# Router weights made at the last projection and in the first mixture, and the first tile's router work in steps between the last products, in a two-layer decoder trunk

## Chip, cores and metric

One core of a Trainium2 chip runs the whole program. The metric is the device time of one execution in microseconds, lower is better. TensorE (PE) multiplies; its weight loads are listed as PEld. VectorE is DVE, ScalarE is ACT, GpSimd is POOL, SyncE is SP. Each engine takes its instructions strictly in the order in which they stand in the program; SP does nothing here but issue the large transfers, one after the other, each when the buffer it writes is free.

## What is computed

The trunk has two layers over 256 tokens of width 2048, in float32. This is the reference, cut to what matters here:

```python
h = x
for layer in range(2):
    m = retention_conv_mixer(h, ...) if layer == 0 else dsa_mixer(h, ...)   # input projection, mixing, output projection
    h = layer_norm(ALPHA * h + m, mix_ln_g[layer], mix_ln_b[layer])
    f = grouped_moe(h, router_w, router_b, w_gu[layer], w_down[layer])
    h = layer_norm(ALPHA * h + f, ffn_ln_g[layer], ffn_ln_b[layer])

def grouped_moe(x, ...):
    affinity = sigmoid(x @ router_w)                 # 256 x 16: the router
    # best of 4 groups of 4 experts, two experts in it, their affinities scaled to sum 1: gate
    for e in range(16):
        a, b = split(x @ w_gu[e], 2)
        y += gate[:, e] * ((silu(a) * b) @ w_down[e])
```

`router_w` (2048 x 16) is shared by both layers. The layer norm before the router is folded into it: with z the unnormed rows, the router's input is rs * (z @ W) + bias, where W is `router_w` scaled row by row with the layer's `mix_ln_g`, less the mean of each column (so that the mean of z drops out), and the bias is `mix_ln_b @ router_w`. W and the bias are the "router weights" of a layer.

## The kernel before

**Stages.** In order: `even` (input projection of layer 0 with rotary embedding, retention and a 31-tap convolution beside it, then the output projection), `moe(0)` (the first mixture), `odd` (layer 1's projections and sparse attention), `moe(1)`, `final` (last layer norm and stores). Tokens are two tiles of 128 rows, t = 0 and 1.

**Projections.** A projection's weights come in chunks of 1 MB (tiles `w`). A chunk is cut into two units of 128 x 1024 values; `split` makes of each a high half on ACT (line 243) and a low half by a subtraction (line 246, tile `sp`) that stands alternately on DVE and POOL, and `mm` issues three products for each of its two slices and two row tiles (lines 284 to 286): 12 products a unit. `dense` walks the units; `ensure` issues the split of a unit three units ahead of its products. After each unit, `bg` issues pieces of background tasks, as many as a budget of 1.3 allows; a task yields its cost (the convolution's steps, line 525, cost 0.33 each, so about four a unit) or -1, which parks it until the next unit. The last five units (`tail`) are done apart: all products of row tile 0, then `z_done` for it, then the products of row tile 1.

**The router's part.** `router(layer)` made a layer's router weights as a background task: in `even` behind the small loads, in `odd` behind the task that turns rows back. It took a page of 8 KB a partition (`rtmp`), loaded `router_w` into it, multiplied it on DVE with both vectors (line 444), summed over the partitions by a product with ones on PE (`prw`, line 447), and reduced, scaled and subtracted on DVE (lines 450 to 453) into `rw`. Each finished column group of an output projection is turned (`psz`, line 734), copied by ACT (`zt`, line 736) and multiplied with `rw` (`plog`, line 739) by `raw`; `total` sums the partial results (`part` on ACT, line 745; `plg` on PE, line 747; `arg` on DVE, line 748). `moe_begin` is called once in the tail, behind the third of the five units of row tile 1, and does for row tile 0 the last `raw`, the norm (`normed`, lines 772 to 778) and `total` in one go.

**The mixtures.** Experts go in eight pairs i, each as `gu(i, 0)`, `down`, `gu(i, 1)`, `down`: 24 chunks a pair, 192 in all (201 MB). SP issues a chunk when one of the pages of its ring (up to 20) has been read to the end.

**The end.** `final` makes six of the eight output pieces on PE and ACT (tile `res`, line 1499) and two on DVE (tile `z`, line 1503); SP stores each.

Of the kernel before, what the change touches and what calls it, by code (L numbers as in the profile page):

```python
# [10 lines left out]
F32 = mybir.dt.float32  # L11
# [69 lines left out]
class Trunk:  # L81
# [208 lines left out]
    def dense(self, us, between, hooks=None, budget=1.3, ahead=3, tail=5):  # L290
        hooks = hooks or {}
        n = 0
        def ensure(i):
            nonlocal n
            while n < min(len(us), i + min(ahead, i + 3) + 1):
                self.split(us[n])
                for f in hooks.get(("split", n), ()):
                    f()
                n += 1

        for i, u in enumerate(us[:-tail]):
            for f in hooks.get(("pre", i), ()):
                f()
            ensure(i)
            self.mm(u)
            if u["last"]:
                u["g"].done(u["g"].acc)
            for f in hooks.get(i, ()):
                f()
            self.bg(budget)  # L310

        for i, u in enumerate(us[-tail:]):
            ensure(len(us) - tail + i)
            self.mm(u, (0,))
        u["g"].done(u["g"].acc, (0,))
        for i, u in enumerate(us[-tail:]):
            self.mm(u, (1,))
            if i == 2:
                between()
        u["g"].done(u["g"].acc, (1,))  # L320


# [61 lines left out]
    def load_small(self):  # L384
# [15 lines left out]
        def task():  # L400
            for _ in range(10):
                yield -1
            ps = self.psum("psv")
            nc.tensor.transpose(ps[:, 0:P], v, self.ident)
            nc.tensor.transpose(ps[:, P:P + 24], cv, self.ident[:24, :24])
            nc.vector.tensor_copy(self.vecs, ps[:, 0:P])
            nc.vector.tensor_copy(self.cvec, ps[:, P:P + 24])
            ps2 = self.psum("psw").rearrange("p (c t) -> p c t", c=16)
            for c in range(8):
                nc.tensor.transpose(ps2[:, c, :TAPS], cw[:, c * P:(c + 1) * P], self.ident[:TAPS, :TAPS])  # L410
            nc.vector.tensor_copy(self.cw[:, :, :TAPS], ps2[:, 0:8, :TAPS])
            nc.gpsimd.partition_broadcast(self.gng, self.gng[0:1, :])
            self.pool_split = True
            yield 0.6
            nc.gpsimd.dma_start(self.cst[:, P:], self.a["c_misc"][:, P:])
            nc.gpsimd.tensor_copy(self.tri, self.cst[:, C_TRI:C_TRI + P])
            nc.gpsimd.tensor_copy(self.identb, self.ident)
            self.ret = self.page("ret", [P, R_N])
            nc.gpsimd.dma_start(self.ret, a["c_ret"])
            nc.gpsimd.dma_start(self.rb, a["router_b"].rearrange("(o e) -> o e", o=1).to_broadcast([P, 16]))  # L420

            for l in range(2):
                for n, nm in enumerate(("mix_ln_g", "mix_ln_b")):
                    nc.gpsimd.dma_start(self.vp[:, 2 * l + n, :].rearrange("p (q r) -> p q r", q=8), a[nm][l].rearrange("(q p r) -> p q r", p=P, r=2))
            yield -1
            yield from self.router(0)
        self.tasks.append(task())

    def router(self, layer):

        nc = self.nc
        V = nc.vector
        tmp = self.page("rtmp")
        raw = tmp[:, 0:256].rearrange("p (k e) -> p k e", k=16)
        both = tmp[:, 256:768].rearrange("p (n k e) -> p n k e", n=2, k=16)
        sums = tmp[:, 768:800].rearrange("p (n e) -> p n e", n=2)
        one = tmp[:, 1024:1024 + P]
        nc.gpsimd.dma_start(raw, self.a["router_w"].rearrange("(c p) e -> p c e", p=P))
        nc.gpsimd.memset(one, 1.0)
        for _ in range(6):  # L440
            yield -1
        for n in range(2):
            v = self.vecs[:, 32 * n + 16 * layer:32 * n + 16 * layer + 16]
            V.tensor_tensor(both[:, n], raw, v[:, :, None].to_broadcast([P, 16, 16]), ALU.mult)
        yield -1
        ps = self.psum("prw")
        nc.tensor.matmul(ps, one, tmp[:, 256:768], start=True, stop=True)
        yield -1
        for n in range(2):
            V.tensor_reduce(sums[:, n], ps[:, n * 256:(n + 1) * 256].rearrange("p (k e) -> p e k", k=16), AX.X, ALU.add)  # L450
        V.tensor_copy(self.rbias, sums[:, 1])
        V.tensor_scalar(sums[:, 0], sums[:, 0], 1.0 / D, None, op0=ALU.mult)
        V.tensor_tensor(self.rw[:, :, 0:16], both[:, 0], sums[:, 0][:, None, :].to_broadcast([P, 16, 16]), ALU.subtract)
        self.drop()
        yield 0.6

    def halves(self, name):

# [3 lines left out]
    def even(self):  # L462
# [218 lines left out]
        def close_act():  # L681
            est.close()
            self.moe_open(0)
            self.rings(11)
            self.table(AF.Sigmoid)
        hooks = {("pre", n): [start_out], n + 0: [ret_T(0, 0)], n + 1: [ret_T(0, 1)], n + 2: [ret_T(1, 0)],
# [54 lines left out]
    def total(self, t):  # L741

        nc = self.nc
        part = self.mp.tile([P, P], F32, name="part", tag="gtt", bufs=2)
        nc.scalar.activation(part, self.pl[:, t * P:(t + 1) * P], AF.Copy)
        pg = self.psum("plg")[:, 0:16]
        nc.tensor.matmul(pg, part, self.sel, start=True, stop=True)
        nc.vector.scalar_tensor_tensor(self.arg[:, t, :], pg, self.rs[:, t:t + 1], self.rbias, op0=ALU.mult, op1=ALU.add)
# [135 lines left out]
        self.pl = self.psum("plog")  # L884
        self.extra_at = self.first[layer] + 8

    def moe_begin(self):

        self.flush()
        for _ in self.raw(0, 3):  # L890
            pass
        self.normed(0)
        self.total(0)

    def moe(self, layer, before_last=None):
        nc, tc = self.nc, self.tc
# [2 lines left out]
        X, Y, GT = {}, {}, {}  # L899
        self.rings(20)  # L900
        h = self.acc
        for _ in self.raw(1, 3):
            pass
        self.total(1)
        self.route(mp)
        self.gate_parts()

# [194 lines left out]
        for i in range(8):  # L1102
# [31 lines left out]
            def general():  # L1134
                self.overflow(layer, rv, h, wide)
                self.ringmax = 8
                if before_last:
                    before_last()
            also = {6: {1: late((1, 0)), 3: late((1, 1)), 5: late((1, 2)), 7: late((1, 3))},
                    7: {3: general, 5: lambda: begin(2, self.bank), 7: lambda: begin(3, self.psum)}}.get(i)  # L1140
            sl = gu(i, 1, also)
            if i == 6:
                self.drop(2)
# [54 lines left out]
    def odd(self):  # L1198
# [38 lines left out]
                yield -1  # L1237
            self.drop(2)
        self.tasks.append(back())
        self.tasks.append(self.router(1))  # L1240

        t4 = lambda n: ap.tile([P, 2, 512], F32, name=n, tag="t4", bufs=3)
        held = {}
# [222 lines left out]
    def final(self):  # L1466
# [26 lines left out]
        for n, (t, c) in enumerate(shared):  # L1493
# [3 lines left out]
            nc.tensor.matmul(ps[t, c], diag[:, t * P:(t + 1) * P], self.acc[t][:, cut(c)], start=False, stop=True)  # L1497
            o = res[t][:, cut(c)]
            nc.scalar.activation(o, ps[t, c], AF.Copy)
            nc.sync.dma_start(orow[:, t, cut(c)], o)  # L1500
        for t, c in own:
            z = centre(t, c)
            V.scalar_tensor_tensor(z, z, self.rs[:, t:t + 1], b[:, cut(c)], op0=ALU.mult, op1=ALU.add)
            nc.sync.dma_start(orow[:, t, cut(c)], z)

    def build(self):
        self.setup()
# [30 lines left out]
```

## Time and profile before

| | us |
|---|---|
| device time, median of 3 runs (lowest to highest) | 1684.91 (1682.84 to 1686.29) |
| the profiled execution: its own time | 1684.84 |
| its span, first to last instruction | 1683.1 |
| busy in the span: PE / DVE / ACT / POOL | 1634.3 / 793.7 / 528.5 / 359.6 |

The profile is of one execution; 1.74 us of its time lie outside the span. Busy time of PE is modelled from pipelined products and says little of what bounds a stage. The views used below are what the 16 DMA engines moved in slices, tables of stretches, the chain of work that ended last, lists of instructions in order of time, and tables of who waited for whom.

### The profile page before, as it was taken

Reading aid. Unit: us, or ns where it says so; the run is one execution under the profiler, and the core shown is the slowest. Engines: PE = TensorE matmul, PEld = TensorE weight load, DVE = VectorE, ACT = ScalarE, POOL = GpSimd, SP = SyncE. Lnnn points to the kernel's source line nnn. Section 1 sums busy time; section 2 is a strip of 40 time slices with the busy share of each in tenths; the row PEclk is TensorE's granted clock in tenths of the full one; section 3 lists DMA queues with packets and bytes.
Section 4 is the critical chain, followed back from the end, with each engine's and each line's share of the span. In section 5 each row is a group of like instructions: output and inputs, shape, how many; then the busy total and the mean of one; then the engine's idle time right before and its main releaser. Section 6 shows DMA issues by size and latency. Waiting matters only on the chain.

```text
span 1683.1 us, 21370 instructions
## 1 busy us (share of the span) xinstructions
PE 1634.3 (97%) x8449; PEld 1021.2 (61%) x8449; DVE 793.7 (47%) x1467; ACT 528.5 (31%) x852; POOL 359.6 (21%) x247
## 2 busy tenths in 40 slices
PE   9999999998999999999999999999899999999998
PEld 7877887786344444544347788878645444454534
DVE  5699987723132223335246585664313322322624
ACT  5333445443121211121135444554312221212112
POOL 2444554542000000010013544334200000001000
PEclk9999999999999999999999999999999999999999
DMA  9754545948999999999993553447789999999994
GB/s 345 220 175 151 175 134 170 339 172 325 355 411 424 427 426 426 427 426 426 425 331 127 167 183 127 149 151 275 315 343 427 417 427 426 426 426 427 427 425 187
DMA packets 123165, 528.47 MB, mean 314 GB/s; under 512 B 10651, under 2 KB 11171, under 8 KB 74803
## 3 DMA queue, kind: packets, MB, share of 16 engines
q1 hardware_dynamic: 122130, 525.32, 79.3%
q0 software_dynamic: 784, 1.66, 0.4%
q8 instruction: 69, 1.13, 0.3%
q14 instruction: 38, 0.30, 0.0%
q10 hardware_dynamic: 144, 0.07, 0.0%
HBM read 524.91 MB, written 2.10 MB: 313 GB/s over the span
## 4 chain that ended last, share of the span: by engine, by line
PE 80%; DVE 8%; DMA 6%; ACT 3%; issue 1%; POOL 1%; DVEq 0%; ACTq 0%; POOLq 0%; SPq 0%
PE pgu L956 22%; PE pdn L1000 11%; PE acc L284 10%; PE acc L286 10%; PE acc L285 9%; PE psg L916 7%; DMA w<-in_moe_w_gu_dram 4%; PE psa L1019 3%; DVE pcv L525 3%; DMA w<-in_moe_w_down_dram 2%; DVE sp L246 2%; PE pdn L1087 1%; PE acc L263 1%; ACT sp L243 1%; DVE Yl L990 0%
## 5 line engine op out<-in xcount | busy, mean ns | idle before, releaser
L956 PE MATMUL pgu<-w,X 128*64 128x512 f32 x2048 | 451.4, 594 | 2.9 <-DMA w<-in_moe_w_gu_dram 2.9
L246 POOL TENSOR_TENSOR sp<-w,sp 128x1024 fp32r<-128x1024 f32 (+1 forms) x105 | 262.7, 2510 | 295.1 <-ACT sp L243 274.7
L956 PEld LDWEIGHTS pgu<-w,X 128*64 128x64 f32 x2048 | 144.2, 137 | 289.5 <-issue 268.3
L243 ACT ACTIVATE sp<-w 128x1024 fp32r<-128x1024 f32 (+1 forms) x224 | 226.4, 1045 | 104.9 <-PE acc L286 36.2
L246 DVE TENSOR_TENSOR sp<-w,sp 128x1024 fp32r<-128x1024 f32 (+1 forms) x119 | 182.1, 1535 | 138.2 <-ACT sp L243 137.1
L1000 PE MATMUL pdn<-w,gT 128*64 128x512 f32 x944 | 209.1, 595 | 0.0
L990 DVE SCALAR_TENSOR_TENSOR Yl<-pdn,gs,Yh 64x512 fp32r<-64x512 f32 (+1 forms) x124 | 90.8, 733 | 228.8 <-ACT Yh L989 215.1
L989 ACT ACTIVATE Yh<-pdn,gs 64x512 fp32r<-64x512 f32 (+1 forms) x124 | 82.9, 668 | 230.3 <-PE pdn L1000 171.5
L284 PE MATMUL acc<-sp,xhi 128*128 128x512 f32 x384 | 153.2, 399 | 0.0
L285 PE MATMUL acc<-sp,xhi 128*128 128x512 f32 x384 | 150.8, 393 | 1.8 <-DVE sp L246 1.8
L286 PE MATMUL acc<-sp,xlo 128*128 128x512 f32 x384 | 150.4, 392 | 0.0
L1000 PEld LDWEIGHTS pdn<-w,gT 128*64 128x64 f32 x944 | 65.3, 137 | 121.6 <-issue 116.7
L874 POOL CAST pb<-pt 128x256 bf16<-128x256 f32 x16 | 7.0, 436 | 611.7 <-DVE pt L873 506.4
L960 DVE TENSOR_TENSOR sl<-sl,pgu 128x256 f32<-128x256 f32 x32 | 13.5, 421 | 243.1 <-ACT sl L959 243.1
L959 ACT ACTIVATE sl<-pgu 128x256 f32<-128x256 f32 x32 | 12.3, 383 | 358.4 <-PE pgu L956 358.4
L525 DVE SCALAR_TENSOR_TENSOR pcv<-up,cw,pcv 128x255 f32<-128x255 f32 (+14 forms) x240 | 113.1, 471 | 7.3
L923 DVE TENSOR_SCALAR X<-psg,vp 128x128 f32<-128x128 f32 x128 | 52.4, 410 | 107.0 <-ACT X L925 107.0
L284 PE MATMUL acc<-sp,hhi 128*128 128x512 f32 x240 | 99.1, 413 | 0.4 <-ACT hhi L1223 0.4
L286 PE MATMUL acc<-sp,hlo 128*128 128x512 f32 x240 | 93.9, 391 | 0.0
L285 PE MATMUL acc<-sp,hhi 128*128 128x512 f32 x240 | 93.6, 390 | 0.0
L925 ACT ACTIVATE X<-psg,vp 128x128 f32<-128x128 f32 x128 | 58.5, 457 | 99.5 <-PE psg L916 68.8
L285 PEld LDWEIGHTS acc<-sp,xhi 128*128 128x128 f32 x384 | 72.5, 189 | 17.8 <-DVE sp L246 3.1
(332 smaller groups left out, 2224.1 us busy)
## 6 DMA issues: line engine op xcount, KB each, us to landing
w<-in_moe_w_gu_dram SPq DMA_DIRECT2D x256, 1024.0 KB, 18.9
w<-in_moe_w_down_dram SPq DMA_DIRECT2D x126, 1024.0 KB, 19.4
w<-in_even_w_in_dram SPq DMA_DIRECT2D x46, 1024.0 KB, 6.4
w<-in_odd_w_in_dram SPq DMA_DIRECT2D x32, 1024.0 KB, 5.3
w<-in_even_w_out_dram SPq DMA_DIRECT2D x16, 1024.0 KB, 7.5
w<-in_odd_w_out_dram SPq DMA_DIRECT2D x16, 1024.0 KB, 5.1
acc<-in_x_dram SPq DMA_DIRECT2D x8, 256.0 KB, 8.5
w<-in_even_w_in_dram SPq DMA_DIRECT2D x4, 512.0 KB, 6.0
```

The lines of the kernel that those rows point to most:

```text
L243: nc.scalar.activation(sp[:, 0], src, AF.Copy)
L246: eng.tensor_tensor(sp[:, 1], src, sp[:, 0].bitcast(F32), ALU.subtract)
L284: nc.tensor.matmul(ac, xh[:, x], wh, start=st, stop=False)
L285: nc.tensor.matmul(ac, xh[:, x], wl, start=False, stop=False)
L286: nc.tensor.matmul(ac, xl[:, x], wh, start=False, stop=en)
L525: nc.vector.scalar_tensor_tensor(y, up[:, c, 0:S - i], w, y, op0=ALU.mult, op1=ALU.add)
L916: nc.tensor.matmul(ps[:, b * P:(b + 1) * P], f, self.PT[i][0][:, t, :], start=t == 0, stop=t == 1)
L925: nc.scalar.activation(X[i][:, k, :], ps[:, b * P:(b + 1) * P], AF.Identity, bias=sh, scale=g)
L956: nc.tensor.matmul(ps[h * 64:(h + 1) * 64, :], X[i][:, k, j * 64:(j + 1) * 64], wv[:, kk, :, h, :], start=k == 0, stop=k == KT - 1)
L989: nc.scalar.activation(hi, po[r, :], AF.Copy, scale=g)
L990: V.scalar_tensor_tensor(lo, po[r, :], g, hi.bitcast(F32), op0=ALU.mult, op1=ALU.subtract)
L1000: nc.tensor.matmul(po[b][half * 64:(half + 1) * 64, :], gT[:, c, h * 64:(h + 1) * 64], wv[:, half ^ j, 2 * b:2 * b + 2, :], start=kk == 0, ...
```

## The change

The router's weights are loaded straight into `rw` (in `even` with the other small loads, by POOL; for layer 1 again at expert pair 2 of the first mixture). Layer 0's `router` is now a background task that starts when the output projection has begun and the mixture's buffers are open; layer 1's is called in three steps during `gu(3, 1)` of the first mixture. The page `rtmp` is gone. `between` is called behind each of the five units of the tail, and `moe_begin` issues its work in pieces behind the third and the fourth; `total` of row tile 0 ends in `moe`. In `final` the stores stand in another order.

```diff
@@ dense
         for i, u in enumerate(us[-tail:]):
             self.mm(u, (1,))
-            if i == 2:
-                between()
+            between(i)
@@ load_small
             nc.gpsimd.dma_start(self.ret, a["c_ret"])
+            self.router_load()
             nc.gpsimd.dma_start(self.rb, ...)
...
-            yield -1
-            yield from self.router(0)
@@ router
-        tmp = self.page("rtmp")
-        raw = tmp[:, 0:256].rearrange("p (k e) -> p k e", k=16)
...
-        nc.gpsimd.dma_start(raw, self.a["router_w"].rearrange("(c p) e -> p c e", p=P))
+        raw = self.rw[:, :, 0:16]
+        flat = self.mp.tile([P, 512], F32, name="rboth", tag="gtt", bufs=2)
...
+        one = self.mp.tile([P, 256], F32, name="sl", tag="sl", bufs=1)[:, 0:P]
         nc.gpsimd.memset(one, 1.0)
-        for _ in range(6):
-            yield -1
...
+    def router_load(self):
+        self.nc.gpsimd.dma_start(self.rw[:, :, 0:16], self.a["router_w"].rearrange("(c p) e -> p c e", p=P))
@@ even, close_act
             self.moe_open(0)
+            self.tasks.append(self.router(0))
@@ total
+        yield -1
         part = self.mp.tile([P, P], F32, name="part", tag="gtt", bufs=2)
         nc.scalar.activation(part, self.pl[:, t * P:(t + 1) * P], AF.Copy)
+        yield -1
         pg = self.psum("plg")[:, 0:16]
@@ moe_begin
-    def moe_begin(self):
-        self.flush()
-        for _ in self.raw(0, 3):
-            pass
-        self.normed(0)
-        self.total(0)
+    def moe_begin(self, i):
+        if i == 2:
+            self.flush()
+            self.steps = [self.raw(0, 3), self.total(0)]
+            for g in self.steps:
+                next(g)
+            next(self.steps[0])
+            self.normed(0)
+        if i == 3:
+            next(self.steps[0], None)
+            next(self.steps[1])
@@ moe
-        for _ in self.raw(1, 3):
-            pass
-        self.total(1)
+        next(self.steps[1], None)
+        for g in (self.raw(1, 3), self.total(1)):
+            for _ in g:
+                pass
...
+            if layer == 0 and i == 2:
+                self.router_load()
...
+            if layer == 0 and i == 3:
+                steps = self.router(1)
+                also = {c: lambda: next(steps, None) for c in (1, 4, 6)}
             sl = gu(i, 1, also)
@@ odd
-        self.tasks.append(self.router(1))
@@ final
-            nc.sync.dma_start(orow[:, t, cut(c)], o)
+        for k in shared[:2]:
+            store(*k)
         for t, c in own:
...
             nc.sync.dma_start(orow[:, t, cut(c)], z)
+            for k in shared[2 + 2 * t:4 + 2 * t]:
+                store(*k)
```

PE in the tail of the first output projection, before: the products `acc` of row tile 1, and between the third unit and the fourth `psz`, `plog` and `plg` of row tile 0 (`acc_70` is row tile 0, `acc_71` row tile 1).

```order
L286 MATMUL acc<-sp,cclor 128x512
L734 MATMUL psz<-cst,acc_70 128x128 x4
L739 MATMUL plog<-zt,rw 32x128 x4
L747 MATMUL plg<-cst,part 128x16
L284 MATMUL acc<-sp,cchir 128x512
...
L286 MATMUL acc<-sp,cclor 128x512
L734 MATMUL psz<-cst,acc_71 128x128 x4
```

The same place now.

```order
L731 MATMUL psz<-cst,acc_70 128x128 x4
L284 MATMUL acc<-sp,cchir 128x512
...
L286 MATMUL acc<-sp,cclor 128x512
L736 MATMUL plog<-zt,rw 32x128 x4
L284 MATMUL acc<-sp,cchir 128x512
...
L286 MATMUL acc<-sp,cclor 128x512
L746 MATMUL plg<-cst,part 128x16
L731 MATMUL psz<-cst,acc_71 128x128 x4
```

Six products of the fourth unit now stand between `psz` and `plog`, six of the fifth between `plog` and `plg`, and the tail of the second output projection is changed in the same way.

DVE where the convolution begins, before: the subtractions `sp`, the router's work on `rtmp`, and the convolution's steps on `pcv`.

```order
L246 TENSOR_TENSOR sp<-w_378,sp 128x1024
L444 TENSOR_TENSOR rtmp<-rtmp,vecs 128x256 x2
L527 TENSOR_SCALAR pcv<-up,cw,cvec 128x256 x2
L525 SCALAR_TENSOR_TENSOR pcv<-up,cw,pcv 128x255 x2
L246 TENSOR_TENSOR sp<-w_439,sp 128x1024
L450 TENSOR_REDUCE rtmp<-prw 128x16 x2
L451 COPY rbias<-rtmp 128x16
L452 TENSOR_SCALAR rtmp<-rtmp 128x16
L453 TENSOR_TENSOR rw<-rtmp 128x16x16
L525 SCALAR_TENSOR_TENSOR pcv<-up,cw,pcv 128x254 x2
...
L246 TENSOR_TENSOR sp<-w_471,sp 128x1024
```

The same place now.

```order
L246 TENSOR_TENSOR sp<-w_378,sp 128x1024
L523 TENSOR_SCALAR pcv<-up,cw,cvec 128x256 x2
L521 SCALAR_TENSOR_TENSOR pcv<-up,cw,pcv 128x255 x2
L246 TENSOR_TENSOR sp<-w_437,sp 128x1024
L521 SCALAR_TENSOR_TENSOR pcv<-up,cw,pcv 128x254 x2
...
L521 SCALAR_TENSOR_TENSOR pcv<-up,cw,pcv 128x251 x2
L246 TENSOR_TENSOR sp<-w_469,sp 128x1024
```

The router's seven instructions have left this stretch, and the convolution stands two steps further on at the next subtraction.

ACT some 40 us later, where the first finished pair of convolution channels (`pcv`) is copied to `cy`, before.

```order
L499 ACTIVATE sg<-acc 128x512 x2
L243 ACTIVATE sp<-w_687 128x1024
L243 ACTIVATE sp<-w_729 128x1024 x2
L529 ACTIVATE cy<-pcv 128x512
L243 ACTIVATE sp<-w_769 128x1024 x2
```

The same place now.

```order
L495 ACTIVATE sg<-acc 128x512 x2
L243 ACTIVATE sp<-w_678 128x1024
L243 ACTIVATE sp<-w_720 128x1024
L525 ACTIVATE cy<-pcv 128x512
L243 ACTIVATE sp<-w_720 128x1024
```

The copy to `cy` has moved ahead of one high half of a split.

## Rows read from the trace of the kernel before

**Rows 1.** The page: the span, and what the DMA engines moved in 40 equal slices of it.

```profile
span 1683.1 us, 21370 instructions
GB/s 345 220 175 151 175 134 170 339 172 325 355 411 424 427 426 426 427 426 426 425 331 127 167 183 127 149 151 275 315 343 427 417 427 426 426 426 427 427 425 187
```

**Rows 2.** Table of stretches at the start of the first mixture, and one row at the start of the second: length, busy time of PE, PEld, DVE, ACT and POOL with counts, granted TensorE clock (1.00 is 2.4 GHz), share of the DMA engines, GB/s.

```profile
416.00:420.00 4.00, 4.00 (x25) 4.00 (x24) 1.18 (x6) 0.91 (x2) 0.00 (x0) 0.63 1.01 428
420.00:424.00 4.00, 4.00 (x22) 1.46 (x20) 1.10 (x3) 0.91 (x2) 0.00 (x0) 1.00 0.49 184
424.00:428.00 4.00, 4.00 (x28) 2.63 (x28) 0.69 (x2) 0.91 (x2) 0.00 (x0) 1.00 0.97 365
476.00:480.00 4.00, 4.00 (x22) 1.29 (x19) 2.25 (x3) 2.19 (x4) 0.00 (x0) 1.00 0.91 342
...
1222.00:1226.00 4.00, 4.00 (x21) 1.44 (x20) 0.96 (x3) 0.91 (x2) 0.00 (x0) 1.00 0.52 197
```

**Rows 3.** The chain of work that ended last, near the end of the first mixture: start, length, what.

```profile
778.06 21.09 DMA w<-in_moe_w_gu_dram
...
818.73 19.55 DMA w<-in_moe_w_gu_dram
```

**Rows 4.** The same chain in the tail of the first output projection.

```profile
386.38 0.57 PE plog L739 x16
...
400.60 0.23 PE acc L286
400.83 0.45 PE psz L734 x4
401.30 0.60 ACT zt L736
401.90 1.40 ACT acc L776 x2
403.30 0.17 ACT part L745
403.52 0.40 PE plg L747 x2
403.91 0.33 PE acc L284
406.79 0.70 DVE acc L719
```

**Rows 5.** The same chain in the tail of the second output projection.

```profile
1203.76 1.40 ACT z L776 x2
```

**Rows 6.** DVE in order of time where the convolution begins: start, length, instruction, count, and in brackets the idle time before it and what ended it.

```profile
57.39 0.69 DVE L500 TENSOR_TENSOR sg<-sg,ga 128x512 f32<-128x512 f32 x1 [0.67 <-ACT sg L499]
61.78 0.75 DVE L444 TENSOR_TENSOR rtmp<-rtmp,vecs 128x256 f32<-128x256 f32 x2
65.76 2.51 DVE L246 TENSOR_TENSOR sp<-w,sp 128x1024 fp32r<-128x1024 f32 x1 [0.26 <-ACT sp L243]
68.19 0.74 DVE L450 TENSOR_REDUCE rtmp<-prw 128x16 f32<-128x256 f32 x2
70.67 2.51 DVE L453 TENSOR_TENSOR rw<-rtmp 128x256 f32<-128x256 f32 x1
73.11 3.08 DVE L525 SCALAR_TENSOR_TENSOR pcv<-up,cw,pcv 128x254 f32<-128x254 f32 x6
```

**Rows 7.** DVE, POOL and ACT in order of time, 30 us further on (three lists, one after the other), and last the subtractions on DVE from 66 to 114 us as one group: count, busy time in us, mean ns of one, idle time before them.

```profile
103.86 5.69 DVE L500 TENSOR_TENSOR sg<-sg,ga 128x512 f32<-128x512 f32 x2
113.31 1.22 DVE L246 TENSOR_TENSOR sp<-w,sp 128x1024 fp32r<-128x1024 f32 x1
...
103.70 5.30 POOL L246 TENSOR_TENSOR sp<-w,sp 128x1024 fp32r<-128x1024 f32 x2 [10.90 <-ACT sp L243]
...
116.41 0.60 ACT L529 ACTIVATE cy<-pcv 128x512 f32<-128x512 f32 x1 [10.89 <-DVE pcv L525]
...
L246 DVE TENSOR_TENSOR sp<-w,sp 128x1024 fp32r<-128x1024 f32 x8 | 12.3, 1533 | 0.3 <-ACT sp L243 0.3
```

**Rows 8.** Who waited for whom, PE alone, 40 to 400 us: us in total, times, the longest.

```profile
PE psq L590 <- POOL qr L710: 3.1, 4, 1.0
PE acc L285 <- DVE sp L246: 1.4, 1, 1.4
PE psq L590 <- POOL qr L711: 0.5, 2, 0.2
```

**Rows 9.** Table of stretches, columns as in rows 2, just behind the second of the waits for POOL.

```profile
159.00:163.00 4.00, 4.00 (x14) 3.22 (x14) 3.82 (x8) 1.09 (x2) 2.07 (x1) 0.57 0.19 22
```

**Rows 10.** Table of stretches, columns as in rows 2, while the second load of `router_w` runs beside the weights of layer 1's projection.

```profile
870.00:872.00 2.00, 1.80 (x7) 0.84 (x6) 1.32 (x3) 1.55 (x3) 0.01 (x1) 1.00 1.05 409
872.00:874.00 2.00, 2.00 (x6) 0.76 (x5) 0.00 (x0) 0.17 (x1) 0.00 (x0) 1.00 1.09 395
874.00:876.00 2.00, 2.00 (x9) 1.20 (x8) 0.54 (x1) 0.78 (x2) 0.00 (x0) 1.00 0.99 278
```

**Rows 11.** The chain that ended last, at layer 1's `prw` in `odd`.

```profile
899.71 0.86 PE prw L447 x2
```

**Rows 12.** The end: the chain's last row, and SP's last stores in order of time.

```profile
1677.29 0.60 ACT res L1499
...
1678.34 0.89 SPq L1504 DMA_DIRECT2D out_dram<-z  x2
```

More of the change, by code (lines that the diff above doesn't have):

```diff
@@ L432, in router @@
         V = nc.vector
-        tmp = self.page("rtmp")
-        raw = tmp[:, 0:256].rearrange("p (k e) -> p k e", k=16)
-        both = tmp[:, 256:768].rearrange("p (n k e) -> p n k e", n=2, k=16)
-        sums = tmp[:, 768:800].rearrange("p (n e) -> p n e", n=2)
-        one = tmp[:, 1024:1024 + P]
-        nc.gpsimd.dma_start(raw, self.a["router_w"].rearrange("(c p) e -> p c e", p=P))
+        raw = self.rw[:, :, 0:16]
+        flat = self.mp.tile([P, 512], F32, name="rboth", tag="gtt", bufs=2)
+        both = flat.rearrange("p (n k e) -> p n k e", n=2, k=16)
+        sums = self.mp.tile([P, 2, 16], F32, name="rsum")
+        one = self.mp.tile([P, 256], F32, name="sl", tag="sl", bufs=1)[:, 0:P]
         nc.gpsimd.memset(one, 1.0)
-        for _ in range(6):
-            yield -1
         for n in range(2):
@@ L446, in router @@
         ps = self.psum("prw")
-        nc.tensor.matmul(ps, one, tmp[:, 256:768], start=True, stop=True)
+        nc.tensor.matmul(ps, one, flat, start=True, stop=True)
         yield -1
@@ L453, in router @@
         V.tensor_tensor(self.rw[:, :, 0:16], both[:, 0], sums[:, 0][:, None, :].to_broadcast([P, 16, 16]), ALU.subtract)
-        self.drop()
-        yield 0.6
+    def router_load(self):
+        self.nc.gpsimd.dma_start(self.rw[:, :, 0:16], self.a["router_w"].rearrange("(c p) e -> p c e", p=P))
     def halves(self, name):
@@ L1499, in final, with store @@
             nc.scalar.activation(o, ps[t, c], AF.Copy)
-            nc.sync.dma_start(orow[:, t, cut(c)], o)
+        def store(t, c):
+            nc.sync.dma_start(orow[:, t, cut(c)], res[t][:, cut(c)])
+        for k in shared[:2]:
+            store(*k)
         for t, c in own:
```

## The prediction, made before the changed kernel ran

> **What bounds the kernel now.** I read the page's slices first. In two long rows of slices, about 460 to 840 and 1260 to 1640 us, the DMA engines move a steady 420 to 428 GB/s: the two mixtures [rows 1]. Near the first one's end the chain of work that ended last lies on three transfers of weights of some 20 us each, one behind the other [rows 3], so that mixture ends when its transfers do. It doesn't follow that its beginning is worth nothing. In the table of its first stretches the engines move 428 GB/s until 420, then 184, then 365, and still only 342 just before 480 [rows 2]; from there on the slices are full. Until then SP waits for PE to free pages, so whatever brings PE's start forward brings the whole stream forward, as long as what is gained is less than the transfers' idle time there. Of that, 420 to 424 alone holds (428 - 184) / 428 x 4 = 2.3 us, 424 to 428 another 0.6 and 476 to 480 another 0.8 [rows 2]; the last of these gaps is what counts, since before it all freed pages had been filled. The second mixture begins in the same way: 197 GB/s from 1222 to 1226 [rows 2]. Ahead of the mixtures PE sets the pace, with DVE close behind: in the table of waits PE waits 1.4 us for a DVE subtraction and 3.1 + 0.5 us for POOL's rotary work, which itself follows DVE's [rows 8].
>
> **The change, part by part.**
>
> *Layer 0's router leaves the convolution.* On DVE it held 0.75 us at 61.78 and all from 68.19 to 73.11, 4.92 us, of which the last multiply took 2.51 [rows 6]. The first piece stood where DVE waited for its next input anyway, I count it as nothing. Of the 4.92, two convolution steps of 3.08 / 6 = 0.51 each now stand ahead of the next subtraction, which leaves 3.9 us; that subtraction may still wait for POOL's, so I take 3.2 us. So DVE reaches the two multiplies at 103.86 about 3 us earlier, before their inputs are ready; there they took 5.69 us together, beside POOL's subtractions that began at 103.70, where one alone took 0.69 [rows 6, 7]. Done before POOL begins, they give another 2 to 4 us, less what DVE now waits for ACT. So the subtraction at 113.31, for which PE waited 1.4 us, should be ready some 4 us earlier, and DVE should go into the rotary work of the next groups 4 to 6 us earlier. The waits of [rows 8] sum to 5.0 us; I take 4.7 as gone, because PE, once it is 3 us ahead itself, uses up most of DVE's lead by the last of them. Bounds: 0 (DVE gains nothing) and 5.0. Right behind that last wait the granted clock was 0.57 on average for 4 us, that is, half clock for 3.4 of them, at a cost of (1 - 0.57) x 4 = 1.7 us [rows 9]. After the other waits of that size it did not fall, so I can't say that the wait is its whole cause: I take 1.0, bounds 0 and 1.7. **Sum: -5.7 us**, between 0 and -6.7. The mixture follows in full, because its first transfers wait for pages that these projections free.
>
> *Its new place* in the output projection has the same `prw`, 0.86 us on PE if priced by the row of layer 1 [rows 11], as in the old place: 0. PE could wait there for DVE's two multiplies, issued a unit (12 products) earlier; a unit hides them.
>
> *The tail.* Before, PE turned the last piece (`psz`, done at 401.28), stood until ACT had copied it (401.90), multiplied, stood until ACT had done two norms and `part` (403.47), multiplied `plg`, and went on with products at 403.91 [rows 4]. That is 403.91 - 401.28 = 2.63 us, and 0.10 for a first product of 0.33 where a running one takes 0.23. Now six products, 6 x 0.23 = 1.4 us, follow `psz` at once: ACT's copy (0.60) is ready when they end. `plog` stays on the path: eight products, half of the sixteen that took 0.57, and 0.1 for the restart on either side, 0.5 us together [rows 4]. `plg` comes behind the last product, where PE waits 0.70 us for DVE's sum anyway; without that cover it would cost its 0.40 [rows 4]. **Saved: 2.73 - 0.5 = 2.2 us**, bounds 1.5 and 2.7. The second tail has the same row, ACT's two norms at 1.40 us [rows 5]: **-4.4 us** for both. Row tile 0's `arg` now comes behind row tile 1's sum and moments on DVE; nothing needs it before row tile 1's own `arg`, which waits for PE later still. The gaps named above (2.3 + 0.6 + 0.8 among them) are larger than 2.2, so the transfers pass it on.
>
> *Layer 1's router in the first mixture.* The load of `router_w` ran before beside a projection's weights: the engines moved 409 GB/s, then 395 and 278 for 2 us each [rows 10], so (14 + 131) x 2 / 409 = 0.7 us were lost, and its own 131 KB, contained in these rates, take 0.3 more. In the old place PE set the pace; in the new one the engines are full, so the stream ends **1.0 us later**, bounds 0.3 (its bytes alone) and 2. `prw` and a wait for DVE's multiplies, which stand behind four `Yl`, may hold PE up to 2.5 us; that is hidden, because the mixture ends with transfers that PE waits for [rows 3]. If PE were late there, it would cost that much. DVE's and POOL's pieces are the same few us as before, on engines with room there.
>
> *Layer 1's `prw` leaves `odd`*, where it stood on the chain: **-0.9 us** [rows 11].
>
> *The stores.* The last `res` is ready at 1677.29 + 0.60; both `z` pieces, though finished earlier, were issued behind it and took SP 0.89 us from 1678.34 [rows 12]. Now the last `res` is the last store: **-0.8 us**, bounds 0 and 0.9.
>
> Together -5.7 - 4.4 + 1.0 - 0.9 - 0.8 = -10.8 us, against the profiled execution's 1684.84: 1674.0 us. Its time is 0.07 us below the median of the three runs, so no correction is due.
>
> **The rivals.**
>
> *A. As above, 1674 us.* Its own range is 1670 to 1678: the convolution's term between -3 and -6.7, the others not all at one end of their bounds at once. Chance 0.50.
>
> *B. The convolution gains nothing: 1679.7 us.* DVE is busy almost without a break there, and a second queue, POOL's, sets when rotary work is ready; the order could fall back into the same lag. Against it speaks that the removed 4.92 us are plain in the list. Chance 0.19.
>
> *C. More than that: 1669 us.* At the start of each mixture PE's clock is at half (0.63 from 416 to 420 [rows 2]); if the shorter idle time ahead spares part of it, 1 to 2 us come off each. Chance 0.07.
>
> *D. The tails are absorbed:* transfers already queued fill the start of the mixtures, the gaps just close. Then -10.8 + 4.4: 1678.4 us. The gap at 476 to 480 speaks against it. Chance 0.07.
>
> *E. The change doesn't do what it says:* neither the lag nor the tails move the end, +1.0 - 0.9 - 0.8 stays, 1684.1 us. Chance 0.08.
>
> *F. Slower.* A DVE subtraction took 1.22 us alone and 2.51 beside POOL's [rows 6, 7]. The eight from 66 to 114 us took 12.3 [rows 7]; if all of them, brought forward, fall under POOL's, 8 x 2.51 - 12.3 = 7.8 us come in for the 4.92 that left. The copy `cy` has moved ahead of one high half on ACT, where it waited for the convolution until 116.41 [rows 7]. It would then begin at 119.3, and POOL's subtraction behind it end at 119.3 + 0.60 + 5.30 / 2 = 122.6 or later. PE wanted the subtraction of 113.31 at 113.31 + 1.22 - 1.4 = 113.1 [rows 7, 8] and wants the next a unit (12 x 0.23 = 2.7 us) later, at 115.8: it would stand 6.8 us instead of 1.4, and some 3.4 us at half clock might follow (1.7): +7.1, with two such stretches +8.8. With the other terms' -5.1 this gives 1686.8 to 1688.5 us. From 117.3 us on for that copy nothing is left of the whole gain. For it speaks that the two multiplies at 103.86 suffered so; against it, that the convolution's steps kept 0.51 us while POOL worked [rows 6], and these are most of DVE's work. The Trainium skill (GPSIMD Engine Reference, 1. Specifications) has POOL share its SBUF interfaces with VectorE and contend with DVE instructions that read two SBUF inputs, as the subtractions do; by that rule F is possible wherever both subtract at once, and the trace agrees (2.51 against 1.22 us). Chance of F: 0.09.
>
> **How the numbers follow.** The time is A's, 1674.0. A change within 0.2% (3.4 us) can't be told from none here: faster is below 1681.5, slower above 1688.3. A gives 0.50, B 0.16 of its 0.19, C 0.07, D 0.06: 0.79 faster. E, the rest of B and D, and a third of F: 0.15 the same. The rest of F: 0.06 slower. The range from 1668 to 1682 takes in A, B, C and D and leaves out E and F (0.17) and their neighbours' edges, about 2 in 10.
>
> **What the changed profile would show.** Right: PE's waits between 100 and 165 us gone or under 1 us, no half clock near 155; products following `psz` without a gap in both tails, `psz` (400.83 before) near 395 and DVE's sum behind the last product (406.79 before [rows 4]) near 399; gaps in the transfers from 420 to 480 smaller by 2 us, and a dip of about 1 us in a full stretch near 540; no `prw` in `odd`; the last store issued with the last `res`. Wrong: the copy `cy` later than 116, a wait at `prw` in either new place, the first mixture ending less than 7 us earlier (D), or half-clock stretches that appear where PE was full before.

## The result, and the profile after

| | before | after |
|---|---|---|
| time, median (lowest to highest), us | 1685.51 (1682.84 to 1686.29), 4 runs | 1670.76 (1669.06 to 1671.27), 4 runs |
| ratio, 95% interval | | 0.9913 (0.9896 to 0.9931) |
| profiled execution: time, span, us | 1684.84, 1683.1 | 1669.06, 1667.3 |

The changed kernel is 14.7 us faster by this ratio (11.6 to 17.5). The forecast was 10.8 us, 1674.0, with 1668 to 1682 as the range.

The page of after, span and the GB/s of 40 slices, against [rows 1]:

```profile
span 1667.3 us, 21366 instructions
GB/s 352 218 179 182 171 158 166 322 205 317 384 407 419 427 426 426 427 426 426 424 313 152 154 176 139 138 166 272 322 367 414 425 427 427 426 426 427 427 425 195
```

The long rows of 420 to 428 GB/s are as before: the mixtures still end with their transfers, so the gains lie outside these rows.

PE's waits from 40 to 400 us in after, against [rows 8] (us in total, times, the longest):

```profile
PE psd L556 <- DVE cn L548: 2.3, 2, 1.9
PE psr L663 <- DVE sgt L653: 1.8, 1, 1.8
PE plog L736 <- ACT zt L733: 0.7, 1, 0.7
PE psz L731 <- DVE acc L716: 0.7, 1, 0.7
PE plg L746 <- ACT part L743: 0.5, 1, 0.5
PE psq L586 <- POOL qr L708: 0.2, 1, 0.2
```

Of the 3.1 + 1.4 + 0.5 us there, 0.2 are left. (`psd` and `psr`, transposes of the convolution's normed output and of its gated product, had nearly the same waits before, 2.2 and 1.8 us.) Where DVE's lag came from is seen in the list of its instructions (start, length, instruction), then POOL's and ACT's, against [rows 7]:

```profile
100.60 0.69 DVE L496 TENSOR_TENSOR sg<-sg,ga 128x512 f32<-128x512 f32 x1 [0.16 <-ACT sg L495]
101.96 0.69 DVE L496 TENSOR_TENSOR sg<-sg,ga 128x512 f32<-128x512 f32 x1 [0.67 <-ACT sg L495]
106.40 1.22 DVE L246 TENSOR_TENSOR sp<-w,sp 128x1024 fp32r<-128x1024 f32 x1
...
102.95 2.39 POOL L246 TENSOR_TENSOR sp<-w,sp 128x1024 fp32r<-128x1024 f32 x1 [10.29 <-ACT sp L243]
...
108.58 0.60 ACT L525 ACTIVATE cy<-pcv 128x512 f32<-128x512 f32 x1 [4.76 <-DVE pcv L521]
```

The two multiplies now stand ahead of POOL's subtraction and take 0.69 us each instead of 5.69 together; the subtraction of 113.31 is at 106.40, 6.9 us earlier; the copy `cy`, on which rival F hung, is at 108.58 instead of 116.41.

The first tail on PE in after, in order of time, against [rows 4]; the second row of `psz` is row tile 1's:

```profile
391.43 0.60 PE L731 MATMUL psz<-cst,acc 128*128 128x128 f32 x4
391.79 0.48 PE L284 MATMUL acc<-sp,cchir 128*128 128x512 f32 x1
...
393.36 0.42 PE L736 MATMUL plog<-zt,rw 128*32 128x128 f32 x8
393.71 0.50 PE L284 MATMUL acc<-sp,cchir 128*128 128x512 f32 x1
...
395.20 0.29 PE L746 MATMUL plg<-cst,part 128*128 128x16 f32 x2
396.15 0.66 PE L731 MATMUL psz<-cst,acc 128*128 128x128 f32 x4 [0.65 <-DVE acc L716]
```

The two `psz` before:

```profile
400.67 0.60 PE L734 MATMUL psz<-cst,acc 128*128 128x128 f32 x4
407.54 0.66 PE L734 MATMUL psz<-cst,acc 128*128 128x128 f32 x4 [0.78 <-DVE acc L719]
```

From one `psz` to the other it is 4.72 us now and was 6.87. From `psz` to the first product behind `plg` PE stood, before, on ACT twice; now products follow both `psz` and `plog` without a gap.

SP and ACT at the end, against [rows 12]:

```profile
1661.58 0.40 SPq L1518 DMA_DIRECT2D out_dram<-z  x1
1662.08 1.13 SPq L1512 DMA_DIRECT2D out_dram<-res  x2
...
1662.25 0.60 ACT L1509 ACTIVATE res<-pso 128x512 f32<-128x512 f32 x1 [0.26 <-PE pso L1507]
```

The last two stores are of `res`, 0.36 us behind the end of the last copy (1663.21 against 1662.85); before, the last store ended 1.34 us behind it.

To place gains and losses I paired the instructions of PE in two traces and took the difference of their starts. The table holds it in us, against the kernel before, at the first paired instruction from the time given (the time is that of before). "Again" is a second session of the changed kernel, the next three are experiments told below.

| at, before | what lies between | after | again | convolution alone | gate from PSUM | tails alone |
|---|---|---|---|---|---|---|
| 64 | | +0.2 | +2.0 | +0.4 | +0.5 | +2.3 |
| 100 | old `prw` | -0.8 | +1.1 | -0.5 | +0.5 | +2.3 |
| 116 | stop for DVE's `sp` | -2.5 | -0.6 | -2.2 | -1.3 | +2.3 |
| 134.5 | first stop at `psq` | -4.9 | -3.0 | -4.6 | -3.7 | +2.7 |
| 159.5 | second stop at `psq` | -7.2 | -5.3 | -6.9 | -3.8 | +2.2 |
| 164.5 | half clock of [rows 9] | -8.8 | -6.9 | -8.4 | -5.3 | +0.7 |
| 283.5 | | -8.8 | -6.9 | -8.4 | -3.6 | +2.4 |
| 290.5 | `psd` | -10.1 | -8.3 | -8.2 | -3.3 | +2.6 |
| 330 | new `prw` | -9.2 | -7.4 | -7.3 | -3.3 | +2.6 |
| 419 | first tail | -11.1 | -10.0 | -7.2 | -3.1 | +0.6 |
| 560 | load of `router_w` | -10.7 | -10.0 | -7.0 | -2.9 | +0.6 |
| 700 | layer 1's `prw` | -9.5 | -8.8 | -7.0 | -2.9 | +0.6 |
| 895 | end of mixture | -11.3 | -9.1 | -7.2 | -3.8 | -0.3 |
| 905 | `prw` in `odd` | -12.2 | -9.9 | -7.1 | -3.7 | -0.3 |
| 1198 | | -12.7 | -10.5 | -7.0 | -4.8 | -1.5 |
| 1207 | second tail | -14.9 | -12.6 | -7.0 | -4.1 | -3.6 |

The +2.0 and +2.3 at 64 are scatter: in some executions PE waits near 56 us for a POOL subtraction (1.6 us in "again", which is the same kernel as after, and 1.7 in the tails alone). Between 134.5 and 283.5 the last column moves by 2.0 us one way and 1.7 the other, where nothing was edited, so one row of one column is no evidence by itself.

### The profile page after: what moved, and what is told of

Its sections match the earlier page's. It is cut to its first block, busy times and chain, and to the rows that moved or that the text cites. A ratio compares the mean times of both kernels' runs of the same rounds, so it can differ in the third digit from the quotient of the medians.

```text
span 1667.3 us, 21366 instructions
## 1 busy us (share of the span) xinstructions
PE 1629.0 (98%) x8449; PEld 1019.7 (61%) x8449; DVE 783.9 (47%) x1467; ACT 529.0 (32%) x852; POOL 361.4 (22%) x247
## 6 DMA issues: line engine op xcount, KB each, us to landing
w<-in_moe_w_gu_dram SPq DMA_DIRECT2D x256, 1024.0 KB, 17.5
```

## The experiments

Each was timed beside the kernel before on the same chip; the times of before there were 1685.27, 1684.66 and 1685.11 us in the three sessions (first to fourth, fifth to eighth, last three runs).

**The tails alone.**

```diff
 # before, with total() in steps as in the change
-            if i == 2:
-                between()
+            between(i)
```

> The kernel before with the two tails of the output projections in steps, and nothing else of the change. Theory (the prediction's term, and what the starts of PE's instructions in the two traces show: 2.1 and 2.2 us won across the tails): both tails pass on in full, 4.3 us less than the kernel before, 1681.2 us against its 1685.5. Rival D (queued transfers fill the start of the mixtures and the gaps just close): 0 to 1 us less. Rival G (the tails are worth more because the clock at the start of the mixtures also moves): 6 us less or more.

Measured: 1679.18 us, ratio 0.9966 (0.9953 to 0.998), 5.7 us less (3.4 to 7.9). In the table the tails bring 2.1 (2.6 to 0.6, first) and 2.2 (-1.45 to -3.61, second). Rival D falls; G can't be told by the time alone, but at the tails the trace shows no more than the theory.

**The convolution alone.**

```diff
 # before; router_load() and the new router() as in the change, old one kept for layer 1
-            yield -1
-            yield from self.router(0)
+            self.tasks.append(self.router(0))   # in close_act
```

> The kernel before with layer 0's router moved to the last projection, its load into the final tile included; layer 1's router stays in odd with its own load, tails and stores are as before. Theory (starts of PE's instructions in the two traces: 1.6 us won near 114, 2.4 near 131, 1.9 near 157, 1.7 of half clock behind it and 1.2 of half clock in the transposes of cn near 286, 0.7 for the old prw, less 0.5 for the new one): 9.1 us less than before, 1676.4 us. The prediction's term: 5.7 us less, 1679.8 us; then the other 3.4 us come from the other parts of the change. Rival B: no change.

Measured: 1677.98 us, ratio 0.9961 (0.9947 to 0.9974), 6.6 us less (4.4 to 8.9); the profiled span is 7.5 us below before's. Between theory and prediction, and B falls. The column shows why: all that lay up to 164.5 is there (-8.4), but PE's clock fell behind `psd` here as it had before, and in after it had not. Stretches of this kernel, then of after (length, PE, PEld, DVE, ACT, POOL, granted clock, DMA, GB/s):

```profile
276.00:280.00 4.00, 2.23 (x15) 2.10 (x16) 2.39 (x3) 1.37 (x4) 0.65 (x1) 0.89 0.00 0
280.00:284.00 4.00, 4.00 (x15) 3.25 (x14) 0.64 (x1) 4.00 (x9) 0.00 (x0) 0.69 0.00 0
```

```profile
276.00:280.00 4.00, 2.54 (x19) 2.32 (x20) 2.08 (x3) 1.68 (x4) 0.35 (x1) 1.00 0.00 0
280.00:284.00 4.00, 4.00 (x20) 3.27 (x19) 0.94 (x1) 4.00 (x9) 0.00 (x0) 1.00 0.06 8
```

0.11 x 4 + 0.31 x 4 = 1.7 us are lost in the first and nothing in the second, behind the same wait of 2.3 us at `psd`.

**The work on DVE put back, and its steps alone.**

```diff
 # after; again() is the old router(0) on a page of its own, without load and prw: the third run
+            yield -1
+            yield from self.again()   # 2 multiplies, 2 reduces, copy, scale, subtract on DVE
 # the fourth run: the same page and yields, none of the seven instructions
```

> The changed kernel, and in the convolution, where layer 0's router stood, seven DVE instructions of the same shapes and the page they stood in, at the same steps of the task, without load and without prw on PE; their results are not used. Theory 1 (DVE's 4.9 us there push everything behind them, and the two multiplies of the gate under POOL's subtractions): the waits, their restarts and the half clock come back, 7 to 9 us more than the changed kernel's 1670.8, so 1678 to 1680 us. Theory 2 (it is the page and the order of the other tasks that the router's steps changed): as long as the next run, and that one slow too. Theory 3 (PE's own prw there started the stops): 1671 to 1673 us.

> The changed kernel, and in the convolution the old router's page and steps without any of its DVE work. Theory 1 (the DVE work is the cause): 1670 to 1672 us, as the changed kernel. Theory 2 (the page, or the order of the other tasks): 1678 to 1680 us.

Measured: 1681.06 us, ratio 0.9972 (0.996 to 0.9983), with the work; 1672.80, 0.9928 (0.9913 to 0.9942), without it. The work alone brings back 7.4 us against the run with the steps, and in the paired starts 9.2 us between 64 and 165 (from 1.6 to 10.8 behind after). The steps alone keep PE within 0.4 us of after up to 160; behind that their profile has a wait of 1.4 us for a POOL subtraction near 212 and half clock behind `psd` (1.7 us), and the interval of their time overlaps with the changed kernel's. So DVE's work is the cause, not the page, not the order of the tasks, and not `prw` on PE, which the third run lacks. The waits of the third run from 40 to 400 us, and two stretches of it:

```profile
PE acc L285 <- DVE sp L246: 2.5, 1, 2.5
PE psd L579 <- DVE cn L571: 2.3, 2, 1.9
PE psq L609 <- POOL qr L730: 1.9, 3, 1.0
PE psr L686 <- DVE sgt L676: 1.8, 1, 1.8
PE psq L609 <- POOL qr L731: 0.5, 2, 0.2
```

```profile
116.00:120.00 4.00, 3.43 (x8) 2.72 (x9) 3.79 (x9) 1.60 (x3) 0.00 (x0) 0.57 0.00 0
160.00:164.00 4.00, 3.61 (x12) 2.98 (x13) 3.75 (x9) 1.20 (x2) 3.10 (x3) 0.60 0.00 0
```

Ahead of 165 us PE's waits sum to 4.9 us, against 5.0 before, but they are shared out otherwise: 2.5 instead of 1.4 at `sp`, 0.5 instead of 1.8 at the first `psq`, and as before at the second. PE's clock falls behind the stop at `sp` and behind the second at `psq`.

**The multiplies without their collision.** The router stays where it was; only one input of the gate's multiplies moves from SBUF to PSUM, the memory into which PE writes its products. There are four such multiplies; the two of [rows 7] stood beside POOL.

```diff
-                    nc.scalar.activation(sg[:, t, :], ac[t], AF.Sigmoid)
-                    nc.vector.tensor_tensor(sg[:, t, :], sg[:, t, :], held[j][:, t, :], ALU.mult)
+                    nc.scalar.activation(ac[t], ac[t], AF.Sigmoid)
+                    nc.vector.tensor_tensor(sg[:, t, :], ac[t], held[j][:, t, :], ALU.mult)
```

> The kernel before with one edit: the sigmoid of the gate is written back into its PSUM bank, and DVE's multiply reads it there, so that it has one SBUF input instead of two. Nothing else of the change. Theory 1 (the two multiplies at 103.86 cost 5.69 us instead of 1.4 because they stand under POOL's subtractions, and this lag of 4.3 us is as much of the cause as the router's 4.9 us of work): multiplies of 0.5 to 0.7 us each there; DVE about 4 us earlier behind them, the waits at 113 and 131 down by half or more: 2 to 6 us less than before, 1679 to 1683 us. Theory 2 (the router's work alone is the cause, and DVE would lie as late behind it without the collision): multiplies shorter, but less than 1 us at the end. Theory 3 (the collision lies elsewhere, the multiplies stay at 2 us or more).

Measured: 1680.72 us, ratio 0.9974 (0.9963 to 0.9986), 4.4 us less (2.4 to 6.2). DVE and POOL in order of time:

```profile
104.31 1.28 DVE L500 TENSOR_TENSOR sg<-acc,ga 128x512 f32<-128x512 f32 x2
109.34 1.22 DVE L246 TENSOR_TENSOR sp<-w,sp 128x1024 fp32r<-128x1024 f32 x1
...
104.15 4.88 POOL L246 TENSOR_TENSOR sp<-w,sp 128x1024 fp32r<-128x1024 f32 x2 [10.89 <-ACT sp L243]
```

Both multiplies run under POOL's subtractions and take 1.28 us instead of 5.69. Theory 1 holds: the stop near 114 and the first at `psq` are gone (the column "gate from PSUM": -1.7, -2.4), the second stays, and the half clock behind it is gone (-1.5). At a wait of 1.3 us for a POOL subtraction at 217, 1.7 us are lost again; the tails alone and the steps alone have such a wait there too. So over half of the convolution's gain hung on this collision, by the times (4.4 of 6.6 us, both with wide intervals) and by the starts at 164.5 (5.7 of 8.9). It was the router's work that had pushed DVE into it: with the convolution alone the two multiplies stand at 100.87 and 102.23 and take 0.69 us each. The Trainium skill (SBUF — State Buffer, SBUF: two separate sides) says that a POOL instruction that reads SBUF and a DVE instruction with two SBUF inputs lock one pair of ports against each other for a whole instruction. The trace agrees to within 0.3 us: with POOL's two subtractions at 2.39 us each alone and the multiplies at 0.69, four instructions taking turns need 6.2 us, and those before took 5.9, from 103.70 to 109.55.

The router's own 4.9 us in the convolution were stretched in the same way. POOL and DVE there before, then DVE in after's first mixture, where no POOL instruction runs beside it:

```profile
64.80 8.11 POOL L246 TENSOR_TENSOR sp<-w,sp 128x1024 fp32r<-128x1024 f32 x3 [4.02 <-ACT sp L243]
68.97 1.59 DVE L451 COPY rbias<-rtmp 128x16 f32<-128x16 f32 x1
```

```profile
608.43 0.76 DVE L445 TENSOR_REDUCE rsum<-prw 128x16 f32<-128x256 f32 x2 [2.54 <-PE prw L442]
609.22 0.17 DVE L446 COPY rbias<-rsum 128x16 f32<-128x16 f32 x1
609.51 0.43 DVE L448 TENSOR_TENSOR rw<-rboth,rsum 128x256 f32<-128x256 f32 x1
```

The same five instructions take 1.5 us there, from 608.43 to 609.94. The copy (1.59 us) and the last subtraction (2.51 us in [rows 6], where the prediction calls it a multiply) end 0.04 and 0.3 us behind POOL's second and third subtraction, which end at 70.52 and 72.90. So some 3.4 of the 4.9 us were standing and not work.

**The load in the mixture, eight times and earlier.**

```diff
             if layer == 0 and i == 2:
-                self.router_load()
+                for _ in range(8):
+                    self.router_load()
```

> The changed kernel with the load of the router's weights in the first mixture issued eight times in a row instead of once. The prediction's term (the stream is full, each load delays the end of the mixture by 1.0 us, bounds 0.3 to 2): 7 more loads are 7 us more (2 to 14), so about 1677.8 us. Rival (the load's cost is made up before the mixture ends, as the two traces suggest, where the first mixture's end moved by as much as its beginning): less than 1.5 us more, and PE's products at the end of the mixture no later.

Measured: 1678.82 us, ratio 0.9957 (0.9945 to 0.997), 8.1 us above after's 1670.76, or 7.4 by the two ratios: 1.1 us for each of seven more. The page's GB/s, against after's above:

```profile
GB/s 343 223 186 184 170 163 152 323 202 322 385 415 409 386 417 427 426 426 426 426 339 126 161 190 126 150 151 276 312 359 425 418 427 426 426 427 427 427 425 186
```

Slices 13 to 15 hold 409, 386, 417 where after has 419, 427, 426: 60 GB/s over a slice of 42 us, 5.9 us of the stream, plus 7 x 131 KB, 2.1 us: 8.0 us. The prediction's term of 1.0 stands. That after's first mixture did not show it is scatter: from the start of the output projection's last product to the mixture's last gate product it takes 442.7, 443.1, 443.5, 443.8, 444.0 and 444.1 us in the six profiles with one load at the third pair of experts, 441.8, 442.2, 442.6, 442.7 and 443.0 in the five without, and 451.0 with eight. The means differ by 1.05 us, though the two groups overlap.

```diff
-            if layer == 0 and i == 2:
+            if layer == 0 and i == 0:
```

> The changed kernel with the load in the first mixture issued at its first pair of experts instead of its third, where the transfers still have gaps. The prediction's term for the load (1.0 us in a full stream): 0.3 to 1.0 us less than the changed kernel, since it falls into a gap. Rival (the load costs nothing where it stands): no difference above 0.3 us.

Measured: 1670.28 us, ratio 0.9913 (0.99 to 0.9925). Too small to tell either way; the mixture took 441.6 us.

**Layer 1's router back in `odd`.**

```diff
-            if layer == 0 and i == 2:
-                self.router_load()
...
+        self.tasks.append(self.router_odd(1))   # the old one, with its own load
```

> The changed kernel with layer 1's router as before, in odd with its own load and prw, and no load in the first mixture. The prediction's terms: plus 0.9 us for prw in odd, less 1.0 us for the load that leaves the mixture: no difference within 0.3 us from the changed kernel, with the first mixture ending 1.0 us earlier. Rival (the load in the mixture costs nothing): the mixture ends as in the changed kernel, and the whole is 0.9 us slower.

Measured: 1670.67 us, ratio 0.9911 (0.9898 to 0.9924), as the changed kernel. That fits the terms (+0.9, -1.0), which pay each other out, but doesn't decide: the rival's 0.9 us lies within the interval, and the mixture, which was to be 1.0 us shorter, took 443.0 us in this profile against 442.7 in after's.

**The changed kernel again, and two steps further.** Two more waits of the list of after are taken away by later steps on PE.

```diff
             yield -1
+            yield -1
             for kp in range(4):
                 ps = self.psum("psd")
 # and in the last run also
-        hooks = {..., n + 0: [ret_T(0, 0)], n + 1: [ret_T(0, 1)], n + 2: [ret_T(1, 0)], n + 3: [ret_T(1, 1), close_act]
+        hooks = {..., n + 1: [ret_T(0, 0)], n + 2: [ret_T(0, 1)], n + 3: [ret_T(1, 0)], n + 4: [ret_T(1, 1), close_act]
```

> The changed kernel itself, unaltered, beside the next two. From the runs so far: 0.9913 of the kernel before, about 1670.5 us. In its first profile PE had no stretch at half clock between 20 and 390 us, where six of the eight other profiles that have no stop at psq show one of 1.7 us behind the stop at psd near 280. Theory (whether the clock falls behind that one stop changes from run to run): this profile may show it or not, and with it the span is 1.5 to 2 us longer.

> The changed kernel with the transposes of cn (psd) one unit of twelve products later, so that DVE's normalization, for which PE waits 2.3 us in all there, is done. Theory (a stop of PE costs its wait, a restart of about 0.3 us, and in most runs the 1.7 us of half clock behind it): 2.5 to 4.5 us less than the changed kernel, 1666 to 1668 us, and no half clock near 280. Rival 1 (the clock falls there whatever PE did before): 2.3 to 2.6 us less, the stretch at half clock stays. Rival 2 (the work behind it, the gated halves at the flush ahead of the output projection, is then as late): no change, with the wait at psr 2 us or more longer.

> The kernel of the run before this one, and the four transposes of the gated product (psr) also one unit later each, since their halves are first read four units on. Theory: the wait of 1.8 us at the first psr and its restart go too, 1.8 to 2.3 us less than the run before, 1664 to 1666 us. Rival (the multiply for which psr waits moves along, or the weights' transfers, whose ring is opened one unit later, come late): no change or up to 2 us more.

Measured, in this order: 1671.13 us, 0.9922 (0.9908 to 0.9935); 1668.75, 0.9905 (0.9888 to 0.9922); 1665.97, 0.9885 (0.987 to 0.99). The second can't be told from the changed kernel by its time, since the intervals overlap. The last beats both kernels: 5.2 us below the changed one in the same session. What is left of PE's wait at `psr` in the second, and in the third:

```profile
PE psr L664 <- DVE sgt L654: 2.9, 1, 2.9
```

```profile
PE psr L664 <- DVE sgt L654: 0.2, 1, 0.2
```

With `psd` alone a unit later, PE came 2.7 us earlier past 290 and lost 1.1 of them at `psr`, which waited 2.9 instead of 1.8: rival 2 in part. With both, PE stands some 3.6 us ahead of the changed kernel at 330, counted from 64, against 1.6 with `psd` alone. The clock did not fall at `psd` in the changed kernel's second profile either, so these runs don't decide rival 1.

## Why the prediction was right, and where its sizes were off

*The convolution, -5.7 us: mechanism right, term too small.* From 64 to 164.5 the changed kernel won 8.9 us (from +0.15 to -8.75), 0.9 of them the old `prw`: 8.0 us, which is outside the bound of -6.7. Two steps of the sum were off.

The first is "the waits of [rows 8] sum to 5.0 us; I take 4.7". In the paired starts the three stops gave 1.7, 2.4 and 2.3 us, 6.4 together. A row of waits counts the time in which PE stood, not how much later its next product starts. PE at the first stop before, then in after:

```profile
130.59 0.39 PE L286 MATMUL acc<-sp,xlo 128*128 128x512 f32 x1
131.45 0.33 PE L590 MATMUL psq<-cst,qr 128*128 128x128 f32 x1 [0.48 <-POOL qr L710]
132.82 0.44 PE L590 MATMUL psq<-cst,qr 128*128 128x128 f32 x2 [1.04 <-POOL qr L710]
133.50 0.77 PE L590 MATMUL psq<-cst,qr 128*128 128x128 f32 x5 [0.25 <-POOL qr L711]
134.02 0.48 PE L284 MATMUL acc<-sp,xhi 128*128 128x512 f32 x1
```

```profile
128.10 0.39 PE L286 MATMUL acc<-sp,xlo 128*128 128x512 f32 x1
128.33 1.03 PE L586 MATMUL psq<-cst,qr 128*128 128x128 f32 x8
129.12 0.48 PE L284 MATMUL acc<-sp,xhi 128*128 128x512 f32 x1
```

From the last product to the next one it is 3.43 us against 1.02: 2.41 us, where the waits are 0.48 + 1.04 + 0.25 = 1.77. The transposes came in three pieces, which took 0.33 + 0.44 + 0.77 = 1.54 us, and in one they take 1.03: that is 0.51 of the 0.64 us that the waits leave out. I also let PE use up part of DVE's lead (4.7 of 5.0); it used up 0.2.

The second is "half clock, 1.0 of 1.7": 1.6 us came off. The three profiles that have the stop at `sp` and both at `psq` show such a stretch behind one of them, or two (before, the tails alone, the work put back). The other ten show none from 20 to 270 us, and one of these, the gate from PSUM, still has the second stop at `psq`. So the half clock goes with the stops, but no one stop brings it each time. A stretch takes 1.7 us in each of these places.

The other 1.3 us at `psd` in after are not the change's: eight of the ten other profiles with that wait have the stretch (the count in the expectation of "again" was wrong), three of them of kernels that are the same as the changed one up to there. The work of the change ends at -8.0; the convolution alone measured -6.6 (4.4 to 8.9).

*The cause.* The prediction had DVE's lag from the router's 4.9 us and from the collision of the two multiplies. The runs show both: the work alone brings back waits of the same sum, its steps don't, and taking only the collision away wins 4.4 us. What the prediction didn't see is that POOL had stretched the 4.9 us as well.

*The new place of layer 0's `prw`, 0:* 0.9 us left at 64 to 100 and 0.9 came back at 312 to 330 (the "new `prw`" row). Right.

*The tails, -2.2 each:* 2.1 in the run that has them alone, and 2.2 from 1198 to 1207 in after. Right; in the time they gave 5.7 (3.4 to 7.9). In after the row at 419 shows 1.9 us for the first, where the two `psz` show 2.15, for PE's clock is at half longer behind it: 5.1 us are lost by it from 396 to 412 against 3.4 from 412 to 420 before. That is the contrary of rival C.

*The load, +1.0:* 1.1 by the run with eight. Right. The hold-up of PE by `prw` in the mixture is 1.2 us (560 to 700) and is made up by the mixture's end, as the prediction said.

*Layer 1's `prw` out of `odd`, -0.9:* 0.8 from 895 to 905. *The stores, -0.8:* 1.34 - 0.36 = 1.0 us from the last copy to the end of the last store. Right.

With 8.0 for 5.7 the sum is -13.1 us. The two sessions of the changed kernel measured -14.7 (11.6 to 17.5) and -13.1 (10.9 to 15.5). A was right, with its first term too small by 2.3 us. B, D, E and F fell: `cy` is at 108.58, and the collision took place before the change, not after it. F's mechanism is there in small. DVE's subtractions from 66 to 114 us in after, against the last of [rows 7]:

```profile
L246 DVE TENSOR_TENSOR sp<-w,sp 128x1024 fp32r<-128x1024 f32 x9 | 15.2, 1686 | 0.3 <-ACT sp L243 0.2
```

Nine at the old mean of 1.53 us would take 13.8, so 1.4 us more stand beside POOL, most of it in one subtraction (2.54 us at 111.16), without a stop of PE behind it.

## What to carry to other kernels

Price a stop of the pacing engine from the start of the last instruction ahead of it to the start of the next one behind it, and not by its waits alone; a stop in three pieces cost 2.4 us for 1.8 of waits. Work on a busy second engine is worth more than its own length where it, or what it pushes back, gets into another engine's way: five DVE instructions that take 1.5 us by themselves took 4.9 beside POOL and cost 8.0 on PE, over half of it through two multiplies that ran into POOL's next subtractions. A term of 1 us in a full stream is not seen in one profile whose length scatters by 1 us either way; repeat the suspected operation until it stands out.

## What the runs showed of the chip beside that

A DVE multiply of 128x512 f32 with one input in PSUM keeps its length beside POOL (1.28 us for two), with both in SBUF two took 5.69. A DVE copy of 128x16 f32 took 1.59 us beside POOL's subtractions and 0.17 without them. A load of 131 KB in rows of 64 bytes costs a stream of 427 GB/s 1.1 us, 0.8 more than its bytes. The time lost by half clock between 20 and 480 us was 3.4, 5.1, 6.8 or 8.5 us in all profiles, that is, two to five stretches of 1.7 us; the same stop at `psd` was followed by one in some executions and not in others.
